# Bias rows stored in half steps from the tenth step of a convolution, residual rows loaded ahead of the second columns, and nine warm-up matmuls in place of seven

## The chip, the cores and the metric

The kernel runs on one core of a Trainium2 chip. Its time is the device time of one launch in microseconds (us). The time before is the median of three runs, 2101.12 us (2098.7 to 2104.93). Two kernels of this case can be told apart from about 0.3%, some 6 us.

A core has engines with a queue of instructions each: TensorE (PE, matrix products; PEld is its weight loads), VectorE (DVE), ScalarE (ACT), GpSimd (POOL) and SyncE (SP), which here issues nearly all DMA transfers. An engine takes its instructions in their order; one that has to wait holds all behind it.

## The reference

A decoder trunk of two layers, for 1024 tokens of width 1024, all in float32. Layer 0 mixes tokens by a causal convolution module; layer 1 by attention over a window of 128 tokens. In each layer, a normalisation follows the mixer and a squared-ReLU MLP follows that, then a gated embedding is added. The part of it that this case is about is the convolution module with the residual sum and the normalisation after it:

```
def conformer_conv(x, w_in, b_in, w_dw, b_dw, ln_g, ln_b, w_out, b_out):
    h = x @ w_in + b_in
    a, gate = jnp.split(h, 2, axis=-1)
    h = a * jax.nn.sigmoid(gate)
    h = lax.conv_general_dilated(
        h, w_dw[:, None, :], window_strides=(1,), padding=[(CONV_WIDTH - 1, 0)],
        dimension_numbers=("NWC", "WIO", "NWC"), feature_group_count=D_MODEL) + b_dw
    h = jax.nn.silu(layer_norm(h, ln_g, ln_b))
    return h @ w_out + b_out
```

CONV_WIDTH is 31. After it comes `layer_norm(ALPHA * x + conv(x), mix_g, mix_b)`, with ALPHA = 4 to the power 0.25. The result of this norm is wanted twice: as the MLP's input, and, times ALPHA, as the MLP's residual, which the kernel keeps in DRAM in eight tiles `mid[0][t]` of 128 tokens. `ALPHA * mix_b` is the constant part of that residual.

## The kernel before, in words

**Products.** Every float32 matrix is split into a high and a low part (`wh`, `wl` of a weight, `xTh`, `xTl` of an activation): ScalarE casts the high part, VectorE subtracts it for the low part, and TensorE sums three products. Matmuls have 128 rows of weights and mostly 512 columns.

**Order.** All operations are first recorded, in the order in which the code calls them. Then `schedule` (line 343) simulates the engines with a table of costs, assumed landing times of transfers (`LANDING`) and slots of named buffers (`SLOTS`), and takes, on each engine, the ready operation that was recorded first; `nc.later(by)` shifts the place of what is recorded within it, and `nc.after(op)` makes it wait for an operation. `issue` then writes out each engine's instructions in the resulting order, all from line 493, so the profile shows L493 everywhere and one goes by tile names. A change in the recorded order or in a wait thus moves the instructions of several engines.

**Convolution.** `conv` records, after `warm_up` (matmuls of a zero tile, `WARM` in number, before the first weight arrives), the loads of x transposed, and then a loop over steps n = 0 to 39. Each step takes one quarter of a channel group of 128 from `ins` (x @ w_in, the gate, and the store of the gated values to DRAM, `scr`), and from step 8 on one quarter from `outs`, which is `taps`: the depthwise convolution. Groups 0 and 1 are plain products (`conv_in`), the rest, `conv_seven`, make seven half products of sums of blocks where there would be eight. `taps` reads `scr` back in shifted form into tiles `z`, and multiplies by banded matrices E that are made from w_dw: a load of 128x576 elements, a cast on ScalarE and a subtraction on VectorE. For every other E the load goes into a slot of the buffer `bo`, of which there are two; for the others into one half of the tile `spread`, which the profile shows as E. Sums go out to DRAM as `zd`.

**The bias rows.** At step n == BIASED the loop loads the rows of mix_b for both layers, in halves of 512, into the same two slots `bo` (`load_row`, each row broadcast to 128 partitions), multiplies them by ALPHA on GpSimd, and stores one partition to `bias[i]` in DRAM. In the steps after it, `bias_rows` copies row `bias[0]` from DRAM to the tiles `mid[0][t]`, broadcast over 128 tokens: 256 KB for each half. Much later `keep_row` adds ALPHA times the normalised values onto `mid` by a DMA that accumulates. SyncE has eight semaphores for its transfers in turn, so a transfer also waits for the landing of the one issued eight before it.

**Behind the convolution.** `conv_stats` and `conv_ln(e, r)` normalise the sums by channel, first columns e = 0 and then e = 1; per e it runs over eight tiles k, and `done[k]` is VectorE's last operation of tile k. `reload(c, e)` brings `zd` back: e = 0 into tiles X, e = 1 into tiles A. `residual(t, xt, op)` loads rows of x (B tiles for t = 0, 1, 4, 5; A for the others) after `op`, and VectorE forms ALPHA * x + b_out. Then `mix_out` multiplies by w_out. The two waits in question, from the end of `conv`, are:

```
        done = conv_ln(0, r)
        with nc.later(ROWS_BY):
            for t, xt in zip((0, 1, 4, 5), rows):
                residual(t, xt, done[XB])
        for c in range(KB):
            with nc.after(done[SECOND]):
                reload(c, 1)
        with nc.later(BEHIND):
            done = conv_ln(1, r)
```

Of the kernel before, what the change touches and what calls it, by code (L numbers as in the profile page):

```python
# [20 lines left out]
NT = T // P  # L21
# [25 lines left out]
BEHIND = 200  # L47
ROWS_BY = 0
BIAS_BY = 200
BIASED = 3  # L50
XB, SECOND = 3, 4
FIRST_OUT = "shifted", 6, 1, 1
PLAIN = 2
ZC = 288
# [27 lines left out]
DOWN = (0, 1, 2), (3, 4), (5, 6, 7)  # L82
SUMMED = (0, 7)
GRAIN = 64
WARM = 7
EARLY = 2
URGENT = 200
PLAN = (
# [439 lines left out]
class Emit:  # L528
# [214 lines left out]
        nc.vector.scalar_tensor_tensor(out=v, in0=v, scalar=ALPHA, in1=g, op0=ALU.mult, op1=ALU.mult)  # L743
        nc.gpsimd.dma_start(self.mid[i][t][:, cols], v, accum_op=ALU.add)

    def bias_rows(self, i, tiles=range(NT)):

        for t in tiles:
            for q in range(2):
                cols = slice(q * HT, (q + 1) * HT)  # L750
                at = np.broadcast_to(np.arange(cols.start, cols.stop), (P, HT))
                src = View(self.bias[i].buf, at, P, (("fn", lambda a, cols=cols: a[:, cols].to_broadcast([P, HT])),))
                self.nc.sync.dma_start(self.mid[i][t][:, cols], src)
# [89 lines left out]
    def warm_up(self):  # L843
# [4 lines left out]
        ps = self.ps()  # L848
        for k in range(WARM):
            nc.tensor.matmul(ps, z[:, 0:P], z, start=True, stop=True)  # L850
# [29 lines left out]
    def conv(self):  # L880
# [190 lines left out]
        def reload(c, e):  # L1071

            Z[c, e] = self.sb("XA"[e])
            src = View(zd[c].buf, np.arange(T), P, (("fn", lambda a: a[:, e * HT : (e + 1) * HT]),))
            nc.sync.dma_start(Z[c, e], src)
# [62 lines left out]
        for n in range(32 + LAG):  # L1138
            next(ins, None)
            if n == ready:  # L1140
                for k in range(4):
                    self.differences(k)
            if n in (ready, ready + 1):
                for j in ((3, 2), (4, 1))[n - ready]:
                    for k in range(4):
                        self.split_form(j, k)
            if n == BIASED:
                for i in range(2):
                    for q, v in enumerate(self.load_row("bo", d["mix_b"][i : i + 1])):
                        nc.gpsimd.tensor_scalar(out=v, in0=v, scalar1=ALPHA, scalar2=0.0, op0=ALU.mult, op1=ALU.add)  # L1150
                        nc.sync.dma_start(self.bias[i][:, q * HT : (q + 1) * HT], v[0:1])
            if BIASED < n <= BIASED + NT:
                self.bias_rows(0, (n - BIASED - 1,))
            if n >= LAG:
                next(outs, None)
            if n == BACK[0]:
                for c in range(BACK[1]):
                    reload(c, 0)
            if n == 30 + LAG:
                last = nc.ops[-1]  # L1160
            if n >= 32 + LAG - 8 // EARLY * EMBEDDED:
                with nc.later(EMBED_BY):
                    for k in range(min(EARLY, 8 * EMBEDDED - HELD - made)):
                        next(early)
                        made += 1
# [1112 lines left out]
```

## Time and profile before

| What | Value |
|---|---|
| median of 3 runs | 2101.12 us (2098.7 to 2104.93) |
| profiled execution | 2099.18 us, its span 2097.5 us, mean granted clock 0.999 |
| TensorE busy | 2078.6 us, 99% of the span |
| VectorE, ScalarE, GpSimd busy | 76%, 55%, 10% |
| chain that ended last | TensorE 88%, VectorE 6%, DMA 2%, ScalarE 2% |
| stores of bias into mid | 32 in the whole program, 256 KB each, 6.8 us from issue to landing |
| DMA engines | mean 217 GB/s, 455.70 MB moved |

The profile is one execution; its own time is 1.9 us below the median. Rows of a timeline give the start, the time that the group was busy, the engine, the instruction with out<-in and shapes, how many, and in brackets the idle time before it and what ended it. Rows of the waits give the total, the number and the longest. SPq is SyncE's queue issuing a transfer; the time there is that of the issue, not of the transfer. For a tile the rows give the minimum, median and maximum in nanoseconds.

The page's last two columns of a table by stretches are the share of time that the DMA engines were busy and the GB/s; the column before is the granted clock of TensorE (PEclk).

### The profile page before, as it was taken

Reading aid. Unit: us, or ns where it says so; the run is one execution under the profiler, and the core shown is the slowest. Engines: PE = TensorE matmul, PEld = TensorE weight load, DVE = VectorE, ACT = ScalarE, POOL = GpSimd, SP = SyncE. Lnnn points to the kernel's source line nnn. Section 1 sums busy time; section 2 is a strip of 40 time slices with the busy share of each in tenths; the row PEclk is TensorE's granted clock in tenths of the full one; section 3 lists DMA queues with packets and bytes.
Section 4 is the critical chain, followed back from the end, with each engine's and each line's share of the span. In section 5 each row is a group of like instructions: output and inputs, shape, how many; then the busy total and the mean of one; then the engine's idle time right before and its main releaser. Section 6 shows DMA issues by size and latency. Waiting matters only on the chain.

```text
span 2097.5 us, 28728 instructions
## 1 busy us (share of the span) xinstructions
PE 2078.6 (99%) x9863; PEld 1731.5 (83%) x9863; DVE 1598.6 (76%) x2502; ACT 1145.6 (55%) x2086; POOL 205.5 (10%) x365
## 2 busy tenths in 40 slices
PE   9999999999999999999999999999999999999998
PEld 7888878888888888888889878878888888888887
DVE  7777798877775768779774798886777656788796
ACT  6566765755555544424433798675555555344343
POOL 0000001000000010000000576110000000100000
PEclk9999999999999999999999999999999999999999
DMA  8878955488868878555777672556888697885526
GB/s 254 264 218 244 323 186 134 145 250 273 266 235 289 253 202 279 186 181 141 244 217 219 214 238 85 141 171 192 255 257 274 205 328 220 222 284 169 163 75 197
DMA packets 232858, 455.70 MB, mean 217 GB/s; under 512 B 22148, under 2 KB 79748, under 8 KB 232712
## 3 DMA queue, kind: packets, MB, share of 16 engines
q1 hardware_dynamic: 223352, 436.83, 63.7%
q0 software_dynamic: 9216, 16.78, 5.1%
q8 instruction: 77, 1.26, 0.3%
q14 instruction: 69, 0.57, 0.1%
q10 hardware_dynamic: 144, 0.26, 0.1%
HBM read 313.27 MB, written 148.91 MB: 220 GB/s over the span
## 4 chain that ended last, share of the span: by engine, by line
PE 88%; DVE 6%; DMA 2%; ACT 2%; issue 1%; POOL 1%; SPq 0%; DVEq 0%; ACTq 0%; POOLq 0%
PE ps L493 67%; PE tr L493 20%; DVE wl L493 1%; DVE A L493 1%; DMA mid<-bias 1%; DVE B L493 1%; ACT z L493 1%; DVE xTl L493 1%; DVE sm L493 1%; DMA raw<-in_w_in_dram 1%; DMA mid<-B 1%; DVE X L493 0%; DVE z L493 0%; ACT t L493 0%; POOL sm L493 0%
## 5 line engine op out<-in xcount | busy, mean ns | idle before, releaser
L493 PE MATMUL ps<-xTh,wh 128*128 128x512 f32 (+1 forms) x672 | 261.9, 391 | 1.2 <-ACT xTh L493 1.2
L493 PE MATMUL ps<-xTl,wh 128*128 128x512 f32 (+1 forms) x672 | 262.4, 391 | 0.2 <-DVE xTl L493 0.2
L493 PE MATMUL ps<-xTh,wl 128*128 128x512 f32 (+1 forms) x672 | 261.8, 390 | 0.3 <-DVE wl L493 0.3
L493 DVE TENSOR_TENSOR wl<-raw,wh 128x1024 fp32r<-128x1024 f32 (+2 forms) x146 | 153.1, 1049 | 101.3 <-ACT wh L493 100.9
L493 PE MATMUL ps<-xTh 128*128 128x512 f32 x552 | 214.7, 389 | 0.0
L493 PE MATMUL ps<-xTl,xTh 128*128 128x512 f32 x552 | 214.7, 389 | 0.0
L493 PE MATMUL ps<-xTh,xTl 128*128 128x512 f32 x552 | 214.7, 389 | 0.0
L493 ACT CAST wh<-raw 128x1024 fp32r<-128x1024 f32 (+2 forms) x146 | 132.0, 906 | 98.4 <-PE ps L493 67.2
L493 ACT CAST wh<-g 128x512 fp32r<-128x512 f32 x152 | 90.0, 620 | 154.5 <-PE ps L493 59.3
L493 ACT CAST xTh<-wh 128x1024 fp32r<-128x1024 f32 x84 | 88.3, 1051 | 152.9 <-PE ps L493 119.1
L493 DVE TENSOR_TENSOR wl<-g,wh 128x512 fp32r<-128x512 f32 x152 | 101.5, 686 | 64.0 <-ACT wh L493 63.3
L493 PE MATMUL ps<-wl,xTh 128*128 128x512 f32 (+1 forms) x400 | 150.1, 376 | 0.0
L493 PE MATMUL ps<-wh,xTh 128*128 128x512 f32 (+1 forms) x400 | 150.0, 376 | 0.0
L493 PE MATMUL ps<-wh,xTl 128*128 128x512 f32 (+1 forms) x400 | 149.4, 375 | 0.2 <-DVE xTl L493 0.2
L493 PEld LDWEIGHTS ps<-xTh,wh 128*128 128x128 f32 x672 | 126.5, 189 | 27.7 <-ACT xTh L493 1.9
L493 PEld LDWEIGHTS ps<-xTh,wl 128*128 128x128 f32 x672 | 126.7, 189 | 26.1 <-DVE wl L493 0.7
L493 PEld LDWEIGHTS ps<-xTl,wh 128*128 128x128 f32 x672 | 126.9, 189 | 24.9 <-DVE xTl L493 0.9
L493 DVE TENSOR_TENSOR xTl<-wh,xTh 128x1024 fp32r<-128x1024 f32 x84 | 102.6, 1221 | 56.8 <-ACT xTh L493 56.6
L493 PEld LDWEIGHTS ps<-xTl,xTh 128*128 128x128 f32 x552 | 103.6, 188 | 21.7
L493 PEld LDWEIGHTS ps<-xTh 128*128 128x128 f32 x552 | 103.6, 188 | 21.5
L493 PEld LDWEIGHTS ps<-xTh,xTl 128*128 128x128 f32 x552 | 103.6, 188 | 21.3
L493 DVE TENSOR_TENSOR xTl<-wl,xTh 128x1024 fp32r<-128x1024 f32 x76 | 92.4, 1218 | 1.7 <-ACT xTh L493 1.7
(398 smaller groups left out, 5056.1 us busy)
## 6 DMA issues: line engine op xcount, KB each, us to landing
wh<-hid SPq DMA_DIRECT2D x84, 512.0 KB, 4.5
raw<-in_w_up_dram SPq DMA_DIRECT2D x67, 512.0 KB, 4.7
wl<-in_w_down_dram SPq DMA_DIRECT2D x58, 512.0 KB, 4.7
hid<-t SPq DMA_DIRECT2D x92, 256.0 KB, 3.6
hid<-zz SPq DMA_DIRECT2D x68, 256.0 KB, 4.3
raw<-hid SPq DMA_DIRECT2D x26, 512.0 KB, 4.2
mid<-bias SPq DMA_DIRECT2D x32, 256.0 KB, 6.8
z<-scr SPq DMA_DIRECT2D x32, 256.0 KB, 4.7
```

Source lines behind the costliest of these rows:

```text
L493: getattr(getattr(nc, o.eng), o.name)(*a, **k)
```

## The change

There are four edits. `WARM` is 9 where it was 7. `BIASED` is 10 where it was 3, so the mix_b rows are recorded at step 10 of the loop instead of step 3. `bias_rows` takes a list of halves, and the loop asks for one half of one tile in each of the 16 steps behind BIASED, where it asked for both halves in each of 8. `XB` is 1 where it was 3, and `SECOND` 6 where it was 4: the B rows of x wait for tile 1 of the first columns' normalisation, and the reloads of the second columns for tile 6.

```diff
-BIASED = 3
-XB, SECOND = 3, 4
+BIASED = 10
+XB, SECOND = 1, 6
...
-WARM = 7
+WARM = 9
...
-    def bias_rows(self, i, tiles=range(NT)):
+    def bias_rows(self, i, tiles=range(NT), halves=(0, 1)):
 
         for t in tiles:
-            for q in range(2):
+            for q in halves:
...
-            if BIASED < n <= BIASED + NT:
-                self.bias_rows(0, (n - BIASED - 1,))
+            if BIASED < n <= BIASED + 2 * NT:
+                self.bias_rows(0, ((n - BIASED - 1) // 2,), ((n - BIASED - 1) % 2,))
```

The arithmetic and the number of transfers are the same. What the scheduler makes of it shows in three places. The first is SyncE's queue early in the convolution, where the two slots of `bo` are first loaded. Before:

```order
L493 DMA bo0_43_107<-in_mix_b_dram 128x512
L493 DMA bo1_44_108<-in_mix_b_dram 128x512
L493 DMA E0_39_103<-in_w_dw_dram 128x576
L493 DMA raw1_318_489<-in_w_in_dram 128x1024
L493 DMA E0_39_103<-in_w_dw_dram 128x576
```

Now:

```order
L493 DMA bo0_43_107<-in_w_dw_dram 128x576
L493 DMA E0_39_103<-in_w_dw_dram 128x576
L493 DMA bo1_44_108<-in_w_dw_dram 128x576
L493 DMA raw1_318_491<-in_w_in_dram 128x1024
L493 DMA E0_39_103<-in_w_dw_dram 128x576
```

The slots of `bo` now take rows of w_dw for the first two E matrices, where they took halves of mix_b.

The second place is SyncE's queue around the next loads of w_dw into `bo`. Before, these are the first ones for the taps, behind the last stores into mid:

```order
L493 DMA mid0_6_123_187<-bias0_264_328 128x512 x2
L493 DMA z2_51_115<-scr0_1_102_166 128x2x256
L493 DMA mid0_7_124_188<-bias0_264_328 128x512
L493 DMA raw0_341_727<-in_w_in_dram 128x1024
L493 DMA mid0_7_124_188<-bias0_264_328 128x512
L493 DMA z3_52_116<-scr0_1_102_166 128x2x256
L493 DMA bo0_338_684<-in_w_dw_dram 128x576
L493 DMA bo1_339_704<-in_w_dw_dram 128x576
L493 DMA raw1_353_801<-in_w_in_dram 128x1024
```

Now the mix_b rows come here; between the two pieces stand seven more stores into mid, of its first halves:

```order
L493 DMA raw0_338_704<-in_w_in_dram 128x1024
L493 DMA bo0_346_752<-in_mix_b_dram 128x512
L493 DMA scr1_0_103_167<-zz0_334_652 512x1x128
L493 DMA scr1_1_104_168<-zz0_334_652 512x1x128
L493 DMA E0_39_103<-in_w_dw_dram 128x576
L493 DMA bias0_264_328<-bo0_346_752 1x512
L493 DMA raw1_355_790<-in_w_in_dram 128x1024
L493 DMA bo1_360_810<-in_mix_b_dram 128x512
L493 DMA mid0_0_117_181<-bias0_264_328 128x512
L493 DMA bo0_356_798<-in_mix_b_dram 128x512
```

```order
L493 DMA bias1_265_329<-bo1_360_810 1x512
L493 DMA scr1_0_103_167<-zz0_351_775 512x1x128
L493 DMA scr1_1_104_168<-zz0_351_775 512x1x128
L493 DMA bias0_264_328<-bo0_356_798 1x512
L493 DMA bo1_369_866<-in_mix_b_dram 128x512
L493 DMA z0_375_892<-scr1_0_103_167 128x2x256
L493 DMA mid0_0_117_181<-bias0_264_328 128x512
L493 DMA bo0_373_888<-in_w_dw_dram 128x576
L493 DMA mid0_1_118_182<-bias0_264_328 128x512
```

The third load of w_dw into `bo`, the row `bo0_373`, stands behind four mix_b loads, three bias stores, and eight first halves and one second half of mid. Its slot is the one that the second half row of mix_b[0] had.

The third place is VectorE's queue at the end of the convolution, where the split of the second w_out tile, `wl0`, stands. Before:

```order
L493 TENSOR_TENSOR B2_709_2813<-B2_709_2813,ps3_777_3132 128x512
L493 TENSOR_TENSOR A2_645_2491<-A2_645_2491,ps4_765_3087 128x512
L493 TENSOR_TENSOR xTl_314_378<-A1_643_2484,xTh_313_377 128x2x2x128
L493 TENSOR_TENSOR A3_648_2508<-A3_648_2508,ps5_762_3064 128x512
L493 TENSOR_TENSOR wl0_775_3128<-raw1_791_3226,wh2_776_3129 128x1024
L493 TENSOR_TENSOR xTl_314_378<-A2_645_2491,xTh_313_377 128x2x2x128
```

Now:

```order
L493 TENSOR_TENSOR xTl_314_378<-X6_656_2544,xTh_313_377 128x2x2x128
L493 SCALAR_TENSOR_TENSOR B5_724_2890<-B5_724_2890,bo0_677_2647 128x512
L493 TENSOR_TENSOR wl0_775_3130<-raw1_791_3228,wh2_776_3131 128x1024
L493 SCALAR_TENSOR_TENSOR B6_727_2903<-B6_727_2903,bo1_670_2601 128x512
L493 TENSOR_TENSOR wl4_792_3234<-raw0_794_3242,wh4_793_3237 128x1024
L493 SCALAR_TENSOR_TENSOR B7_731_2920<-B7_731_2920,bo0_677_2647 128x512
L493 TENSOR_TENSOR A1_643_2486<-A1_643_2486,ps5_762_3066 128x512
```

The split of `wl0` stood between operations of the second columns (tiles A); now it stands between those of the first columns (X) and the residual rows (B), ahead of all work on A1 to A7. TensorE's order is the same but for the two warm-up matmuls and two pieces around these places.

## The prediction

> **What bounds the kernel now.** I read the page's first part, then the waits of the tensor engine, the timelines around its two largest, and the SyncE queue there.
>
> ```profile
> PE 2078.6 (99%) x9863; PEld 1731.5 (83%) x9863; DVE 1598.6 (76%) x2502; ACT 1145.6 (55%) x2086; POOL 205.5 (10%) x365
> ```
>
> TensorE is busy 99% of the span of 2097.5 us. A change can win only what TensorE idles, or spends at a low clock. Its waits, longest first:
>
> ```profile
> PE ps L493 <- DVE E L493: 4.0, 1, 4.0
> PE tr L493 <- ACT wh L493: 1.8, 1, 1.8
> PE ps L493 <- DVE t L493: 1.7, 2, 1.5
> PE ps L493 <- ACT xTh L493: 1.2, 1, 1.2
> PE tr L493 <- DVE wl L493: 0.7, 1, 0.7
> ```
>
> The first row is one wait of 4.0 us for a banded tap matrix E; the second and fifth are one place, where w_out begins; the third and fourth are the start. The timeline of TensorE shows each place, and the clock:
>
> ```profile
> 1.51 3.35 PE L493 MATMUL ps<-t 128*128 128x512 f32 x7 [1.51 <-DVE t L493]
> 6.02 1.22 PE L493 MATMUL ps<-xTh,wh 128*128 128x512 f32 x2 [1.15 <-ACT xTh L493]
> 10.03 0.63 PE L493 MATMUL ps<-xTh,wh 128*128 128x512 f32 x1
> 10.46 0.44 PE L493 MATMUL ps<-xTl,wh 128*128 128x512 f32 x1
> 10.73 0.39 PE L493 MATMUL ps<-xTh,wl 128*128 128x512 f32 x1
> ...
> 61.31 0.39 PE L493 MATMUL ps<-A,wh 128*128 128x512 f32 x1
> 65.68 2.29 PE L493 MATMUL ps<-z,E 128*128 128x256 f32 x9 [3.98 <-DVE E L493]
> 67.77 0.63 PE L493 MATMUL ps<-B,wl 128*128 128x512 f32 x1
> 68.20 0.56 PE L493 MATMUL ps<-B,wh 128*128 128x512 f32 x1
> 68.60 0.39 PE L493 MATMUL ps<-X,wh 128*128 128x512 f32 x1
> ...
> 76.48 1.23 PE L493 MATMUL ps<-z,E 128*128 128x256 f32 x9
> ```
>
> A 512-column matmul starts 0.43 us after the one before it until 10.46, and 0.23 us after from 10.73 on: the low clock costs 0.2 us each. After the wait the clock is low again: 65.68 to 68.60 holds nine matmuls of 256 columns and two of 512, which at the high clock take 9 x 0.12 + 2 x 0.23 = 1.54 us, not 2.92. So that place costs 4.0 + 1.4 us, the start up to 3.
>
> Why E is late stands in the chain of waits and the SyncE queue:
>
> ```profile
> 43.85 10.19 DMA mid<-bias
> ...
> 54.13 7.88 DMA raw<-in_w_in_dram
> ```
> ```profile
> 15.99 0.97 SPq L493 DMA_DIRECT2D bo<-in_mix_b_dram  x2
> ...
> 26.68 1.43 SPq L493 DMA_DIRECT2D bias<-bo  x2
> ...
> 29.29 0.55 SPq L493 DMA_DIRECT2D mid<-bias  x1
> ...
> 35.31 5.12 SPq L493 DMA_DIRECT2D mid<-bias  x6
> ...
> 40.97 3.77 SPq L493 DMA_DIRECT2D mid<-bias  x4
> ...
> 56.14 1.31 SPq L493 DMA_DIRECT2D bo<-in_w_dw_dram  x2
> ```
>
> The mix_b rows take the two slots of `bo` at 15.99, and the sixteen stores of bias into mid hold SyncE; the first two tap loads into `bo` leave at 56.14 only, and the weight load of 54.13, also behind the stores, holds ScalarE.
>
> **Part 1, two more warm-ups.** Seven end at 1.51 + 3.35 = 4.86; two more at 0.43 end near 5.7, before the 6.02 at which the first weights arrive: they delay nothing. Whether they gain depends on what raises the clock: it rose 4.4 us after TensorE's restart at 6.02 and 2.8 us after that at 65.68. Were it up from 6.02 on, (10.46 - 6.02) / 0.43 = 10.4 matmuls would save 0.2 each, 2.1 us; if the clock ignores the warm-ups, 0. The idle in front of 6.02 shrinks from 1.15 to 0.3 us, so I take the upper end less the quarter of the idle that stays, **1.6 us**. [...]
>
> This gain lasts only until TensorE next waits for something that it does not pace, which is part 2.
>
> **Part 2, the bias stores.** The stores at n = 3 go; the tap loads take `bo` at about 16 us, and the first two E matrices are ready long before 61 us. What is late next? The order shows it: the mix_b loads wait for the first taps to be split (DVE), and the third load of taps into `bo` stands on SyncE behind four mix_b loads, three bias stores and nine stores into mid; the matrix it gives is read by TensorE at the work that before did at 76.4 (by adding up the matmuls ahead in both orders, 0.23 and 0.12 us each; before, the group at 76.48 is 0.1 further on). Without any stall TensorE would be there at 61.55 + 9.3 = 70.8, with part 1 at 69.2.
>
> Now the chain, by rows of before:
>
> ```profile
> 30.32 0.75 DVE L493 SCALAR_TENSOR_TENSOR t<-ps,cst,t 128x512 f32<-128x512 f32 x1 [2.15 <-ACT t L493]
> 47.20 0.68 DVE L493 TENSOR_TENSOR X<-X,B 128x512 fp32r<-128x512 f32 x1
> ```
> ```profile
> L493 ACT CAST E<-bo x9: 661/667/677, 64.2 to 105.8; 128x576 fp32r<-128x576 f32 x9
> L493 DVE TENSOR_TENSOR E<-bo,E x9: 746/751/759, 64.9 to 107.6; 128x576 fp32r<-128x576 f32 x9
> L493 POOL TENSOR_SCALAR bo<-bo x4: 620/822/2474, 22.4 to 38.0; 128x512 f32<-128x512 f32 x4
> DMA to landing us min/median/max: 2.7/4.4/7.9
> ```
> ```profile
> L493 SPq DMA_DIRECT2D mid<-bias x16: 469/596/1416, 29.3 to 54.5; - x16
> DMA to landing us min/median/max: 5.5/7.1/10.8
> ```
>
> VectorE is full here; the difference at 47.20 comes 1.6 us earlier (it fills a wait of 2.15 us behind TensorE), and two rows and the split follow: 45.6 + 0.6 + 0.66 + 0.6 + 0.75 = 48.2. Load of mix_b at 48.3, landed 4.4 later (2.7 to 7.9) 52.7, GpSimd 0.82 (to 2.47) 53.5, bias store and its landing 1.9 (27.4 to 29.29) 55.5, a store into mid and a load 0.95: 56.4, seven stores into mid at 0.87 each (5.12/6; 0.6 to 1.4) 62.5, two bias and two gate stores 2.0 (at the 0.5 of a short issue): 64.5, landing of the second bias row (1.9 to 7.1, since it now queues behind eight transfers; I take 4.5) 69.0, one store 0.6: tap load at 69.6, landed 4.4 later 74.0, ScalarE 0.67, VectorE 0.75 and hops 0.2: **75.6**. TensorE waits from 69.2 to 75.6, 6.4 us, and the clock falls as before, 1.4 us (0 to 2.0). Against before: 75.6 + 1.4 - 76.4 = **+0.6 us**. The start's gain is eaten by this wait. The terms' ends combined as independent ones put the arrival between 71.6 and 82.6, so -3.4 to +7.6. All short ends together give 67.3, ahead of TensorE.
>
> The number of stores into mid stays sixteen; seven of the second halves follow the tap load, other loads between them. The next load into `bo` is 15 SyncE rows later (15 x 0.87 = 13 us, 82.6, matrix at 88.6), needed 13.6 us of work after the first: 75.6 + 1.4 + 13.6 = 90.6. Covered by 2 us; where it isn't, that is rival B.
>
> **Part 3, residual rows first.** XB 3 to 1 lets x rows be loaded earlier, SECOND 4 to 6 holds the second columns (A<-zd) back.
>
> ```profile
> 269.85 4.02 SPq L493 DMA_DIRECT2D B<-in_x_dram  x8
> 273.91 4.71 SPq L493 DMA_DIRECT2D A<-zd  x8
> 279.03 0.99 SPq L493 DMA_DIRECT2D raw<-in_w_out_dram  x2
> ```
> ```profile
> 276.45 1.22 DVE L493 TENSOR_TENSOR wl<-raw,wh 128x1024 fp32r<-128x1024 f32 x1
> 291.32 1.22 DVE L493 TENSOR_TENSOR wl<-raw,wh 128x1024 fp32r<-128x1024 f32 x1
> ```
> ```profile
> 290.90 0.50 PE L493 MATMUL tr<-wh,xTh 128*128 128x512 f32 x1 [1.79 <-ACT wh L493]
> ```
>
> In the order the w_out loads move ahead of the eight A<-zd, 4.7 us of issue, so they land about 4.7 us earlier, and the split at 291.32 can run near 286.5, before TensorE is done with its work at 290.90 - 1.79 = 289.1. That gives back both waits of the place, 1.8 + 0.7 = 2.5 us. Against it, the A rows arrive later. VectorE is busy 19.00 of 19 us there:
>
> ```profile
> 275.00:294.00 19.00, 16.49 (x72) 13.03 (x71) 19.00 (x30) 9.27 (x13) 0.00 (x0) 1.00 0.66 248
> ```
>
> so any row that slips must be paid by TensorE later, unless VectorE's residual rows fill the gap, as the order has them do. I take **-2.0 us** (-2.6 to 0, by the waits themselves at one end and a full give-back at the other).
>
> **Sum**: +0.6 - 2.0 = -1.4 us. On the profiled execution's 2099.18 us that is 2097.8. The median of the runs shown is 1.9 us above that execution, so the median to expect is 2101.12 - 1.4 = **2099.7 us**. About 0.3% (6.3 us) is what can be told from no change here; this is well inside.
>
> **Rivals.** A, the tap load is in time: all links of the chain short. For it: the mids' issue has a median of 0.6 us, not 0.87. Against: nine stores of 256 KB just ahead of it, landing in 7.1 us. From an arrival below 69.2 on TensorE never stops: 69.2 - 76.4 - 2.0 = -9.2 us, 2091.9. B, the stores choke the queue: seven at 1.4 us each (+3.7) and the second bias landing at 7.1 (+2.6) put the arrival near 82, 82 + 1.4 - 76.4 = +7.0; the second tap load, 13 us behind one of 75.9 and 7.9 in landing, gives its matrix at 98.4 where 82 + 1.4 + 13.6 = 97.0 is wanted: a second wait of 1.4 and the clock 1.4 again. 7.0 + 2.8 - 2.0 = +7.8 us, 2108.9. For it: the 10.19 in the chain above. Against: the median store of before took 0.6 us on the same queue. It decides from an arrival of 77 (sum zero), and from 81, with the second wait, the kernel is slower by over 0.3%. C, the second columns come too late: with the gain at w_out gone and VectorE idle for 4 us of landing, TensorE loses those: +0.6 + 4.0 = +4.6, 2105.7. Against it stand residual rows of about 0.75 us each as filling.
>
> **How the numbers follow.** Forecast (arrival 71 to 80) 0.53, A 0.22, B 0.18, C 0.07. Range 2093.5 to 2107.5 us: below it lies most of A, above it most of B; the forecast's own range is 2095 to 2104. Faster by over 0.3% (below 2094.8): A less its partial cases, 0.20. Slower by over 0.3% (above 2107.4): most of B, 0.17. Within: 0.63.
>
> **What would show it.** Right: in the changed kernel's waits no stall for E near 61 us but one of 4 to 9 us between 68 and 78, with slow matmuls behind it, mix_b loads near 48 us, the tap load near 70, and the pair of waits at 290 gone. The rise of the clock near 7 shows part 1. Wrong: no wait for E at all before 80 us (A), two of them (B), or VectorE idle between 275 and 300 (C).

## The result, and the profile after

The changed kernel took 2109.27 us (median of six, 2107.53 to 2113.39) where the kernel before, beside it, took 2102.52. The ratio is 1.0036, 95% interval 1.0023 to 1.0048: slower, by about 7.5 us. The forecast was no change, 2099.7; rival B, the stores choking the queue, had 2108.9. The profiled execution after took 2107.53 us, its span is 2105.8, 8.3 more than before.

The waits of TensorE after, in total, count and longest:

```profile
PE ps L493 <- DVE E L493: 14.5, 2, 12.4
PE ps L493 <- DVE xTl L493: 2.0, 2, 1.9
```

The wait of 4.0 us for E, a banded tap matrix, became two, 12.4 and 2.05; the pair at w_out (1.8 and 0.7) is gone, and a wait of 1.9 for `xTl` is new. TensorE's timeline shows their places:

```profile
1.51 4.21 PE L493 MATMUL ps<-t 128*128 128x512 f32 x9 [1.51 <-DVE t L493]
5.52 0.95 PE L493 MATMUL ps<-xTh,wh 128*128 128x512 f32 x2
6.31 0.40 PE L493 MATMUL ps<-xTl,wh 128*128 128x512 f32 x1
...
81.00 2.93 PE L493 MATMUL ps<-z,E 128*128 128x256 f32 x12 [12.42 <-DVE E L493]
83.73 0.63 PE L493 MATMUL ps<-xTh,wh 128*128 128x512 f32 x1
84.16 0.63 PE L493 MATMUL ps<-xTl,wh 128*128 128x512 f32 x1
84.59 0.46 PE L493 MATMUL ps<-xTh,wl 128*128 128x512 f32 x1
...
98.63 3.01 PE L493 MATMUL ps<-z,E 128*128 128x256 f32 x23 [2.05 <-DVE E L493]
...
377.69 0.39 PE L493 MATMUL ps<-xTl,wh 128*128 128x256 f32 x1 [1.87 <-DVE xTl L493]
```

TensorE came to the third `bo` matrix at 81.00 - 12.42 = 68.6 us and got it at 81.0. After the wait the clock was low until 84.6 (granted 0.50 from 81.0 to 84.6): 12 matmuls of 256 columns and three of 512 took 84.89 - 81.00 = 3.9 us, where 12 x 0.12 + 3 x 0.23 = 2.1 is usual, so 1.8 us more. Before did that work at 76.4, so this place costs 81.0 + 1.8 - 76.4 = 6.4 us. The second wait adds 2.05; the 23 matmuls behind it, at a granted clock of 1.00, take 101.48 - 98.63 = 2.85 us, 0.1 more than 23 x 0.12. Together they are 8.5 us; the span grew by 8.3, so the rest of the change adds up to about nothing in this trace.

Why the matrix is late, in SyncE's queue after (start, time of the issue):

```profile
44.42 0.35 SPq L493 DMA_DIRECT2D bo<-in_mix_b_dram  x1
...
51.77 0.56 SPq L493 DMA_DIRECT2D mid<-bias  x1
...
53.01 7.77 SPq L493 DMA_DIRECT2D mid<-bias  x7
60.89 0.56 SPq L493 DMA_DIRECT2D bias<-bo  x1
61.95 3.75 SPq L493 DMA_DIRECT2D scr<-zz  x2
65.82 0.40 SPq L493 DMA_DIRECT2D bias<-bo  x1
70.33 0.36 SPq L493 DMA_DIRECT2D bo<-in_mix_b_dram  x1
72.48 0.39 SPq L493 DMA_DIRECT2D z<-scr  x1
72.96 0.54 SPq L493 DMA_DIRECT2D mid<-bias  x1
73.55 0.58 SPq L493 DMA_DIRECT2D bo<-in_w_dw_dram  x1
```

in its waits between 60 and 76 us:

```profile
SPq L493 <- DMA bias<-bo: 4.0, 1, 4.0
```

and in the chain of work that ended last:

```profile
61.95 10.45 DMA scr<-zz
...
73.55 5.91 DMA bo<-in_w_dw_dram
```

The seven stores take 1.11 us each to issue, the two gate stores (`scr<-zz`) 1.9 each. Then SyncE waits from 66.2 to 70.3: the mix_b load at 70.33 takes the slot whose row was stored at 60.89, and that store of 2 KB has been on its way for over 9 us. The first gate store takes 10.45 us to land, and the reload `z` that waits for it, the row at 72.48, stands ahead of the tap load (the load of w_dw at 73.55).

### The profile page after: what moved, and what is told of

It reads as the page before. It is cut to its first block, busy times and chain, and to the rows that moved or that the text cites. A ratio compares the mean times of both kernels' runs of the same rounds, so it can differ in the third digit from the quotient of the medians.

```text
span 2105.8 us, 28738 instructions
## 1 busy us (share of the span) xinstructions
PE 2079.6 (99%) x9865; PEld 1733.3 (82%) x9865; DVE 1598.4 (76%) x2502; ACT 1148.5 (55%) x2086; POOL 207.1 (10%) x365
## 4 chain that ended last, share of the span: by engine, by line
PE 90%; DVE 3%; DMA 3%; ACT 2%; issue 1%; POOL 1%; SPq 0%; DVEq 0%; ACTq 0%; POOLq 0%
PE ps L493 70%; PE tr L493 21%; ACT z L493 1%; DMA bo<-in_w_dw_dram 1%; DMA mid<-B 1%; DVE wl L493 1%; DMA t<-proj 1%; DMA scr<-zz 0%; DVE xTl L493 0%; DVE A L493 0%; DVE sm L493 0%; DVE z L493 0%; ACT wh L493 0%; DMA raw<-in_w_up_dram 0%; POOL sm L493 0%
## 5 line engine op out<-in xcount | busy, mean ns | idle before, releaser
L493 PE MATMUL ps<-xTl,wh 128*128 128x512 f32 (+1 forms) x656 | 255.0, 389 | 1.9 <-DVE xTl L493 1.9
L493 PE MATMUL ps<-xTh,wh 128*128 128x512 f32 (+1 forms) x656 | 255.1, 391 | 0.2
L493 PE MATMUL ps<-xTh,wl 128*128 128x512 f32 (+1 forms) x656 | 254.8, 389 | 0.3 <-DVE wl L493 0.3
L493 PE MATMUL ps<-wh,xTh 128*128 128x512 f32 (+1 forms) x352 | 132.5, 377 | 0.0
L493 PE MATMUL ps<-wh,xTl 128*128 128x512 f32 (+1 forms) x352 | 132.2, 377 | 0.2 <-DVE xTl L493 0.2
L493 PE MATMUL ps<-wl,xTh 128*128 128x512 f32 (+1 forms) x352 | 132.1, 376 | 0.0
```

Source lines behind the costliest of these rows:

```text
L493: getattr(getattr(nc, o.eng), o.name)(*a, **k)
```

## The experiments

Every ratio is that of a kernel to the kernel before on the same chip, with its 95% interval. Beside these runs the kernel before had medians of 2098.9 to 2099.1 us.

### The bias part alone

```diff
-XB, SECOND = 1, 6
+XB, SECOND = 3, 4
...
-WARM = 9
+WARM = 7
```

> The change's bias part alone (BIASED 10, half steps), with seven warm-ups and XB, SECOND at 3, 4. Theory 1 (the third tap load into bo stands behind the mix_b loads and the mid stores on SyncE): the stall for E at about 68.6 stays, 11 to 13 us for the first and 1 to 3 for a second one, so +7 to +10 us on before, about 2111. Theory 2 (the loss comes from the other two edits): within 2 us of before.

1.0058 (1.0041 to 1.0076). TensorE's timeline has the same wait at the same place, then 2.0 us at 99:

```profile
81.49 2.93 PE L493 MATMUL ps<-z,E 128*128 128x256 f32 x12 [10.91 <-DVE E L493]
```

The bias part alone loses as much as the whole change, or more. In these two profiles TensorE comes to the matrix 2.0 us later with seven warm-ups (70.6 in place of 68.6), and the matrix arrives only 0.5 later, so most of what TensorE lost at the start only shortens its wait.

### Two slots of bo, SyncE's queue, or the traffic

Four kernels take the changed one apart. The first loads mix_b through four other slots, which leaves the slots of `bo` to the taps:

```diff
-                    for q, v in enumerate(self.load_row("bo", d["mix_b"][i : i + 1])):
+                    for q, v in enumerate(self.load_row("g", d["mix_b"][i : i + 1])):
```

> The changed kernel, but the mix_b rows go through slots of the tag g (four slots, those of weight differences) instead of the two of bo, so the third and fourth tap loads no longer wait for a bias row to be stored; the stores into mid stay on SyncE, the DMA traffic is the same. Theory 1: the stall at 68.6 us is gone or under 3 us, 2092 to 2098 us. Rival (the stall is traffic: 4 MB of mid stores slow whatever lands then): the wait for E stays above 8 us, about 2108.

1.0015 (1.0004 to 1.0026), 2102.05 us. The wait at 68.6 is gone, as theory 1 says, but the time lies 4 us above its range: the stores into mid now start behind the fifth tap load, and TensorE waits later instead, as its timeline shows:

```profile
95.69 0.80 PE L493 MATMUL ps<-xTh,wh 128*128 128x512 f32 x1 [2.54 <-ACT t L493]
104.94 2.80 PE L493 MATMUL ps<-z,E 128*128 128x256 f32 x13 [3.63 <-DVE E L493]
```

So the stall moved with the stores. This run moves slots and stores at once and doesn't tell them apart. The second keeps slots and traffic and takes the stores off SyncE:

```diff
-                self.nc.sync.dma_start(self.mid[i][t][:, cols], src)
+                self.nc.gpsimd.dma_start(self.mid[i][t][:, cols], src)
```

> The changed kernel with the 16 stores of bias into mid issued from GpSimd's queue instead of SyncE's; same steps, same slots of bo, same traffic. Theory 1a (SyncE's queue: the tap load stands behind stores that each take 0.5 to 1.4 us to issue and behind a wait for the transfer eight before): the tap load leaves near 62 instead of 73.6 us, the stall at 68.6 shrinks from 12.4 to 0 to 5 us, 2096 to 2103. Theory 1b (traffic: any transfer lands late while 4 MB go from DRAM to DRAM): stall above 8 us, about 2108.

1.0017 (1.0007 to 1.0026), 2103.52 us, with waits of 7.4 and 3.5 us in its profile (an execution of 2106.4 us, slower than its median): between the two theories. The tap load in the chain of waits:

```profile
63.53 10.70 DMA bo<-in_w_dw_dram
```

It left 10 us earlier than in the changed kernel (73.55) and still landed at 74.2, only 5.2 earlier than 79.46: beside the stores it needed 10.70 us. In this kernel a queue free of the stores brings the tap load forward by these 5 us and no more.

The third keeps the slots and steps of mix_b, and holds all full stores back to the end of the convolution:

```diff
-            if BIASED < n <= BIASED + 2 * NT:
-                self.bias_rows(0, ((n - BIASED - 1) // 2,), ((n - BIASED - 1) % 2,))
...
             with nc.after(done[SECOND]):
                 reload(c, 1)
+        with nc.later(300), nc.after(done[7]):
+            self.bias_rows(0)
```

> The changed kernel, mix_b rows still loaded through bo at step 10, but all 16 stores into mid held back until the first columns of the normalisation are done (some 290 us). Theory 1 (the stores into mid): the tap load leaves near 61, no stall for E or one below 2 us, 2093 to 2098. Theory 1c (the two slots of bo, taken by mix_b rows until their bias rows are stored): a stall of 5 us or more stays, above 2101.

0.9956 (0.9944 to 0.9968), 2090.52 us, better than the range. No wait for E is left in its list of waits. Theory 1c falls: mix_b takes the slots of `bo` at the same steps and the tap load leaves at 60.79. The fourth adds to this kernel 16 stores of one row each (`bias_rows` gets the number of rows as its last argument) where the changed kernel has its full ones; the full stores overwrite them later:

```diff
+            if BIASED < n <= BIASED + 2 * NT:
+                self.bias_rows(0, ((n - BIASED - 1) // 2,), ((n - BIASED - 1) % 2,), 1)
...
-                self.nc.sync.dma_start(self.mid[i][t][:, cols], src)
+                self.nc.sync.dma_start(self.mid[i][t][0:n, cols], src)
```

> quiet10 (the full stores into mid at some 290 us) plus 16 stores of one token row, 2 KB each, from bias to mid on SyncE at the places of the changed kernel: its queue without its traffic. Traffic decides: the tap load leaves before 66 us, no stall for E above 1.5 us, within 3 us of quiet10, 2089 to 2094. The queue's issuing decides: the tap load leaves after 70 us, a stall of 5 us or more, 2097 or more.

0.9967 (0.9956 to 0.9979), and again no wait for E. Its SyncE queue:

```profile
44.83 0.34 SPq L493 DMA_DIRECT2D bo<-in_mix_b_dram  x1
...
53.41 4.29 SPq L493 DMA_DIRECT2D mid<-bias  x7
...
63.22 0.58 SPq L493 DMA_DIRECT2D bo<-in_w_dw_dram  x1
```

and its transfers between 44 and 80 us (KB each, median us to landing), then those of the changed kernel:

```profile
bo<-in_w_dw_dram SPq DMA_DIRECT2D x5, 288.0 KB, 3.4
mid<-bias SPq DMA_DIRECT2D x16, 2.0 KB, 2.2
```
```profile
mid<-bias SPq DMA_DIRECT2D x13, 256.0 KB, 7.9
scr<-zz SPq DMA_DIRECT2D x4, 256.0 KB, 6.6
```

From the first mix_b load to the tap load SyncE took 63.22 - 44.83 = 18.4 us with 2 KB stores and 73.55 - 44.42 = 29.1 with 256 KB stores. The instructions between are the same but for `z`, which here stands behind the tap load and has 2.2 us of the difference. What the full stores move decides, not that the queue issues them, and it does so twice: SyncE's issues and the landings that it waits for come late, and then the tap load itself lands late. A store of one row moves fewer rows and fewer bytes, so this run doesn't tell which of the two it is.

### The same with the mix_b rows at step 3, and the start

```diff
-BIASED = 10
+BIASED = 3
```

on the kernel with the stores held back.

> As quiet10, but the mix_b rows loaded at step 3, as in the kernel before, so the taps follow them into bo; XB, SECOND 1, 6 and nine warm-ups stay. Theory 1: no wait for E between 40 and 110 us at all, the start's gain is kept, 2091 to 2095. Rival: the stores at 290 us, beside w_out and the second columns, cost what they save: above 2097.

0.9953 (0.9941 to 0.9965), 2090.15 us: the fastest kernel here, together with the one at step 10, which it can't be told from. Its only wait for E is 0.2 us. The rival of a cost at 290 us isn't seen, as the busy times by stretch (from:to, length, then TensorE's) show; first this kernel, then the one before:

```profile
280.00:300.00 20.00, 20.00 (x90) 16.57 (x89) 19.84 (x30) 10.69 (x15) 0.00 (x0) 1.00 0.81 287
```
```profile
280.00:300.00 20.00, 17.49 (x77) 13.83 (x76) 20.00 (x31) 10.81 (x15) 0.00 (x0) 1.00 0.49 190
```

The DMA engines are busy 0.81 of the time instead of 0.49, and TensorE doesn't wait at all. In this kernel no wait for E behind the start eats a gain at the start, so seven warm-ups in place of nine measure it:

> quiet with seven warm-ups in place of nine: with no wait for E behind the start, the start's gain has nothing to eat it. The prediction's part 1 (1.6 us, more by the trace, where the clock is up at 6.3 in place of 10.46): 1.5 to 2.5 us slower than quiet. [...]

0.9959 (0.9945 to 0.9973), 2090.43 us: no difference that these runs can tell. The medians are 0.3 us apart, less than the 1.5 us expected, but each interval is 2.5 to 3 us to either side, so a gain of 1.6 us isn't excluded. Its profile happens to be one with an early rise. Seven warm-ups have the rise of the clock, from where on 512-column matmuls start 0.23 us apart in place of 0.43, at a different time in each profile: at 10.46 in the kernel before, in the kernel with SECOND 6 alone (below) at 9.5, and here before the first work at 5.77, whose first two matmuls took 0.74 us where the kernel before needed 1.22:

```profile
9.11 0.53 PE L493 MATMUL ps<-xTl,wh 128*128 128x512 f32 x1
9.47 0.39 PE L493 MATMUL ps<-xTh,wl 128*128 128x512 f32 x1
```
```profile
5.77 0.74 PE L493 MATMUL ps<-xTh,wh 128*128 128x512 f32 x2 [0.90 <-ACT xTh L493]
6.49 0.50 PE L493 MATMUL ps<-xTl,wh 128*128 128x512 f32 x1
6.83 0.40 PE L493 MATMUL ps<-xTh,wl 128*128 128x512 f32 x1
```

Over all kernels of this case, the six profiles with seven warm-ups have the rise between 5.4 or earlier and 10.5 us, the eight with nine at 7.7 at the latest. Two more warm-ups thus do go with an early rise in these traces; what that is worth in the median stays below what could be told.

### Nine warm-ups alone

> Nine warm-ups alone on the kernel before. The prediction: the clock rises near 7 us instead of 10.46, TensorE gains 1.6 us or more, and the wait for E at 61 grows by the same, since E's arrival at 65.68 hangs on SyncE and ScalarE: net 0 (-0.5 to +0.5 us). Rival: E's arrival follows TensorE, and the whole 1.6 to 2.5 us stays.

1.0003 (0.9992 to 1.0014). The clock was up at 6.34, TensorE was earlier, and the wait for E came at 59.6 and lasted 3.1 us, up to 62.8. So E didn't stay at 65.68, yet the time is the same. E's arrival moves with or without warm-ups: in the profiles of the next section, with seven, it came at 63.4 to 64.5. This run agrees with the prediction's zero but doesn't show its reason.

### The residual rows

Here the kernel before got XB, SECOND = 1, 6, then each number alone, and the kernel with held-back stores got 3, 4.

> XB, SECOND = 1, 6 alone on the kernel before. Theory 1: the waits of 1.8 and 0.7 us at 290 us go, but the wait of 1.9 us for xTl near 378 with a low clock behind it comes, net -1.5 to +1 us. Theory 2 (this edit makes the loss): +5 us or more. The prediction had -2.0.

Both numbers: 0.9993 (0.9984 to 1.0002).

> The kernel before with XB = 1 alone. Which of the two numbers does what: if the earlier x rows give the gain at w_out, the waits of 1.8 and 0.7 us at 290 us go here; if SECOND does, they stay and the time is within 1 us of before.

XB alone: 1.0014 (1.0005 to 1.0023), 3 us slower, outside what was expected.

> The kernel before with SECOND = 6 alone. If holding back the second columns lets the w_out loads pass ahead of them, the waits at 290 us go here, and the wait for xTl near 378 us, behind mid<-B, comes; net within 2 us of before. If it needs both numbers, the waits at 290 us stay.

SECOND alone: 0.9985 (0.9976 to 0.9994), 3 us faster, outside what was expected.

> As quiet, with XB, SECOND at 3, 4. If the edit of the residual rows is worth nothing in sum, as the pair of waits at 290 us against the wait for xTl near 378 us says, this is within 1.5 us of quiet; if the prediction's -2.0 holds once nothing else stands in the way, it is 2 us slower or more.

The stores held back, with 3, 4: 0.9986 (0.9977 to 0.9994), 7 us slower than with 1, 6.

With XB 1 alone TensorE's two longest waits between 275 and 400 us are these, the first the one at w_out:

```profile
PE tr L493 <- ACT wh L493: 2.9, 1, 2.9
PE tr L493 <- ACT A L493: 1.4, 1, 1.4
```

With SECOND 6 alone the waits at w_out are gone and one of 1.4 us for `xTl` has come, where the kernel before waits 0.2, at 367.8:

```profile
PE ps L493 <- DVE xTl L493: 1.5, 2, 1.4
```

So SECOND lets the w_out loads pass. XB does not: alone it leaves 2.9 us at w_out in place of 1.8 + 0.7. What takes the gain back is in VectorE's timeline of the changed kernel:

```profile
375.42 0.42 DVE L493 TENSOR_TENSOR B<-A,B 128x256 fp32r<-128x256 f32 x1 [2.57 <-DMA mid<-B]
```

VectorE may overwrite a B tile only when GpSimd's accumulating store of it onto mid has ended. Those stores stand later now, since the change moves VectorE's `keep_row` behind other work: before, the first left at 322.22 and three more from 346.56, now the first three from 353.70. VectorE waits 2.57 us, `xTl` is late, TensorE waits 1.87 us and works at a low clock from 378.3 to 381.7 (granted 0.50). In the kernel with held-back stores and 3, 4, the same wait is 4.0 us and TensorE's 3.5, beside the 1.8 and 0.7 at w_out:

```profile
DVE B L493 <- DMA mid<-B: 4.0, 1, 4.0
```

With 1, 6 there it is gone; the first two of these stores leave at 315.2 and 316.4 and the next two from 340.57, not three at once from 353.70. The expectation that this edit has one price was wrong: it was worth 1.5 us on the kernel before (3.4 gained to 0.4 lost), about nothing in the changed kernel's own trace, and 7 us where the stores are held back. Why the order of VectorE's work comes out so well only in that combination stays open.

## Why the prediction was wrong

**What bounds the kernel, and the structure**, were right: the mix_b loads went behind the first taps, the wait for E at 61 went, one for the third `bo` matrix at 68.6 (predicted 69.2) took its place, and the pair at w_out went.

**Part 1** had 1.6 us gained at the start and lost again in the next wait. The clock was up at 6.3, and the gain lost, as it said. Where that wait can't take it, no gain could be told (0.3 us between the medians). The prediction took one execution's late rise, 10.46, for what seven warm-ups do, where the rise came between 5.4 and 10.5 in six profiles. The rise thus varies by some 5 us from profile to profile, and no run shows what sets its time. The rise near 7 that the prediction looked for goes with its estimate of 1.6 us: 1.6 / 0.2 = 8 matmuls, 0.43 us apart, are 3.4 us ahead of 10.46.

**Part 2** is the step that failed: its sum of issues and landings on SyncE's queue, up to the arrival of the third `bo` matrix. The chain from the first mix_b load to the matrix was put at 75.6 - 48.3 = 27.3 us and took 80.96 - 44.42 = 36.5:

| Term | Predicted | Measured |
|---|---|---|
| mix_b load to the first store into mid | 7.2 | 51.77 - 44.42 = 7.4 |
| that store and a load, seven stores | 0.95 + 6.1 | 60.89 - 51.77 = 9.1 |
| two bias, two gate stores, issued | 2.0 | 66.22 - 60.89 = 5.3 |
| a bias row landed | 4.5 | 70.33 - 66.22 = 4.1 |
| to the tap load | 0.6, without `z` | 73.55 - 70.33 = 3.2, with `z` |
| tap load landed | 4.4 | 5.9 |
| cast and split | 1.6 | 1.5 |

It started 3.9 us earlier than predicted and ended 5.4 later. Every term that grew by over 1 us is an issue, a wait or a landing beside the 256 KB stores. Their bounds were taken as independent, and their middles were chosen term by term, but all hang on the same stores, so they were long together. The kernel with 2 KB stores shows it: 18.4 us in place of 29.1, of which `z` has 2.2. One wait was left out: that of `z`, which stands right ahead of the tap load and needs the gate stores landed (10.45 us). And the bias row waited for was not the second, stored at 65.82, but the one stored at 60.89. The clock behind the wait was 1.8 for 1.4. The second wait, which the forecast thought covered by 2 us, came with 2.05. In all +8.5 in place of +0.6. (The sum's own slips are small: 5.12/6 is 0.85, not 0.87.)

**Part 3** had -2.0, with 0 as its other end. In the kernel before it measured 1.5 gained, its interval reaching past zero. In the changed kernel the 2.5 us came, and 1.87 of wait and a low clock took them back. The prediction named VectorE's fullness as the danger, not the accumulating stores that free the B tiles.

**The rivals.** B came true: its mechanism, its second wait, and +8.3 us of span for its +7.8. That the number is so close is partly luck: B had 7.0 for the first place (measured 6.4), 2.8 for the second (2.15) and -2.0 for part 3 (about nothing). Its chance of 0.18 was too low. The argument against it, the median of 0.6 us for the issue of a store, says little: in the changed kernel the median of the sixteen is 0.6 again, and the seven ahead of the tap load took 1.11 each.

**The range** reached to 2107.5, and the time lies above. The forecast's own bounds, to 82.6 for the arrival, held the 81.0; with part 3 at its other end, 0, they reach 2108.7, above the range that was stated.

## What to carry to other kernels

The chain of loads and stores on SyncE's queue was not the sum of its middles: it took 36.5 us where they make 27.3, since the transfers of the chain were the traffic and its terms were long together. So price such a chain at the long end, and look for each wait on a landing in the rows between. Bulk stores that nothing needs soon belong where no load is waited for: with the 16 stores ahead of tap loads the kernel was 7.5 us slower than before, with the same stores at the convolution's end, where the DMA engines had been busy 0.49 of the time (280 to 300 us), 9.2 us faster. The move alone doesn't give that: with XB, SECOND at 3, 4 the kernel with the stores at the end was 2.9 us faster than before, since the waits at w_out stayed and the wait for a B tile grew. After a wait is removed, look for the next instruction that frees a buffer, not only for the next that computes.

## What the runs showed of the hardware

The 256 KB stores from DRAM to DRAM delayed other transfers by more than the busy share of the DMA engines tells. In the kernel with the stores on GpSimd's queue, the stretch in which the tap load of 288 KB took 10.70 us had the engines 0.75 busy and moved 175 GB/s; in the changed kernel, where it took 5.91, they were 0.85 busy and moved 163 GB/s. In the kernel with all 16 stores held back and mix_b at step 10, the same stretch had them 0.76 busy and moved 233 GB/s, and the median of such loads was 3.7 us; with 2 KB stores added it was 3.4 us, at 0.66 and 186 GB/s. The busy times by stretch of the three (the last three columns are the granted clock, the share and the GB/s):

```profile
60.00:76.00 16.00, 8.58 (x47) 7.16 (x46) 5.19 (x9) 4.07 (x8) 5.07 (x11) 0.89 0.75 175
```
```profile
60.00:76.00 16.00, 15.46 (x84) 12.89 (x84) 11.33 (x19) 10.50 (x19) 0.84 (x3) 1.00 0.76 233
```
```profile
60.00:76.00 16.00, 13.98 (x78) 11.70 (x77) 9.72 (x16) 9.08 (x17) 0.84 (x3) 1.00 0.66 186
```

No run here tells what makes it so: that both ends lie in DRAM, that each store reads one row 128 times, or another thing.

In the changed kernel a wait of TensorE of 1.87 us, up to 377.7, was followed by a granted clock of 0.50 from 378.3 to 381.7; behind one of 2.05 us, up to 98.6, the granted clock was 1.00 (98.6 to 101.6).
